# Mask blocks spread between filling units on VectorE, one core of a hybrid attention layer

## The chip, the cores and the metric

The kernel runs on one core of one Trainium2 chip. The metric is device time in microseconds (us) of one execution, lower is better. Engines are called PE (TensorE), DVE (VectorE), ACT (ScalarE), POOL (GpSimd) and SP (SyncE, which here issues every large transfer).

## The reference, cut to what matters

One decoder layer over 1024 tokens of width 1024: an input projection, two parallel attention groups (sliding window, and a sparse group "DSA" whose keys are chosen by an indexer), a cross-attention over 256 memory tokens, and an MLP. The change touches how the choice of keys becomes a mask:

```python
score = jnp.where(causal[None], score, NEG_INF)
_, idx = lax.top_k(score, topk)          # 256 of the keys
ok = idx <= t[None, :, None]
sel = jax.vmap(lambda c, i: c[i])(c_kv, idx)
logits = jnp.where(ok[:, None], logits + bias, NEG_INF)
```

and, beside it in time, the memory's keys and values, which do not depend on the layer's input:

```python
kv = mem @ wkv + bkv
k, v = jnp.split(kv, 2, axis=-1)
```

## The kernel before, in words

The kernel keeps float32 accuracy by splitting each operand of a matmul into a high part and a low part (fp32r) and issuing three matmuls (`mm3`). Weights come through `wload` (lines 148 to 176): a transfer fills a raw buffer `wr` (four of them, 256 KB each), ACT (or POOL) writes the high part into `wh` (line 172), and POOL and DVE, taking turns where `lo=(POOL, DVE)`, write the low part raw minus high into `wl` (line 173). Once both have read it, the raw buffer is free for the next load. One "pair" of memory units shares one `wload`: four raw buffers, of which POOL does the low parts of the first and third, DVE of the second and fourth.

The indexer's scores of six query blocks (n = 2 to 7, of 384 to 1024 keys) lie in `sc`. DVE finds a threshold per row, a rare repair path (`settle_all`, behind a branch) follows, and then `mask_rows` turns each block of scores into an additive mask in place, with five DVE instructions a block (lines 833 to 837): equal to the threshold, a running sum over these (the scan, line 834), at most the threshold, a comparison and a sum. Attention reads `sc` only later (line 965).

While DVE and ACT do this, PE is kept busy by a list `fill` of 60 units: projections `proj_unit` (matmuls `fill<-xT`), small ones `latent_k` (`fill<-cT`), and the memory's `mem_k`, `mem_v` (`fill<-fb,wh` and `fill<-fb,wl`, of 256 columns) and `mem_vo` (`fill<-wh,wt`). A projection's result leaves PSUM through `split_store`: ACT writes its high part (line 444), DVE its low part (line 445) into a `wt` tile (five of them), and SP stores the tile to `qa_d` or `qb_d`; `latent_k` goes through ACT (448, 449), POOL (450) and SP to `kb_d`. The tile is reused when its stores have landed.

The order in which each engine takes its instructions is fixed when the program is built: a scheduler works it out from the data, from the order of the code and from extra order edges. `follow(i, name)` adds such an edge: instruction i is put behind `latest[name]`, without a semaphore. Units 26 to 59 are emitted behind `settle_all` (`CUT = 26`); `mask_rows` is emitted once, ahead of the twentieth of these (`MASKS = 20`), and nothing tells the scheduler where in DVE's order its blocks belong.

Of the kernel before, what the change touches and what calls it, by code (L numbers as in the profile page):

```python
# [17 lines left out]
OP = mybir.AluOpType  # L18
# [9 lines left out]
NEG = -1e30  # L28
# [11 lines left out]
def kernel(ctx: ExitStack, tc: tile.TileContext, x, mem, ln_emb_g, ln_emb_b, w_in, b_in,  # L40
# [4 lines left out]
    PE, ACT, DVE, POOL, SP = nc.tensor, nc.scalar, nc.vector, nc.gpsimd, nc.sync  # L45
    x, mem, out = x[0], mem[0], out[0]
# [19 lines left out]
    def f(ap):  # L66
        return ap.bitcast(F32)
# [3 lines left out]
    def place(pl, names, shape, dt=F32):  # L71

        i = turn[names] = turn.get(names, -1) + 1
        tag = names[i % len(names)]
        return pl.tile(shape, dt, name=tag, tag=tag, bufs=4 if tag in ("wh", "wl", "wr") else 1)
# [63 lines left out]
    latest = {}  # L139

    def follow(i, *names):

        for nm in names:
            if nm in latest:
                tc.add_manual_dep(i.ins, latest[nm].ins.name, NOSYNC, reason="order")

    def wload(src, r0, nk, c0, nc_, hi=(ACT,), lo=(POOL,)):

        wh, wl = [], []
        step = min(nk, 1024 // nc_)  # L150
        for k in range(0, nk, step):
            h, l = (place(pw, w, [P, step, nc_], F32R) for w in (WH, WL))
            r = r0 + k * P
            for i in range(2):
                raw = place(pw, WR, [P, 512])
                if step == 1:
                    ws = slice(i * 512, i * 512 + 512)
                    SP.dma_start(raw, src[r:r + P, c0 + i * 512:c0 + i * 512 + 512])
                    hs, ls = h[:, 0, ws], l[:, 0, ws]
                else:  # L160
                    n2 = step // 2
                    raw = raw.rearrange("p (k c) -> p k c", k=n2)
                    part = src[r + i * n2 * P:r + (i + 1) * n2 * P, c0:c0 + nc_]
                    last_load[:] = [SP.dma_start(raw, part.rearrange("(k p) c -> p k c", p=P))]
                    hs, ls = h[:, i * n2:(i + 1) * n2], l[:, i * n2:(i + 1) * n2]
                eng = hi[i % len(hi)]
                if eng is POOL:
                    POOL.tensor_scalar(hs, raw, 1.0, 1.0, op0=OP.mult, op1=OP.mult)
                elif eng is DVE:
                    DVE.tensor_copy(hs, raw)  # L170
                else:
                    follow(ACT.activation(hs, raw, AF.Copy), "xT")  # L172
                lo[i % len(lo)].tensor_tensor(out=ls, in0=raw, in1=f(hs), op=OP.subtract)  # L173
            wh += [h[:, i] for i in range(step)]
            wl += [l[:, i] for i in range(step)]
        return wh, wl
# [225 lines left out]
    def kdup(pl, src, *names):  # L402
        kk = [place(pl, n, [P, T], F32R) for n in names]
        for hl in range(2):
            for e in range(2):
                SP.dma_start(f(kk[hl])[e * 64:e * 64 + 64], src[hl])
        return kk
# [51 lines left out]
    def proj_unit(c0, nw, cs, bias, scale, dst, t0, n):  # L459
        if cs == 0 and t0 == 0:  # L460
            FW["p"] = wload(w_in, 0, KT, c0, nw, (POOL,))
        split_store(project(*cols(FW["p"], cs), t0, n), bias, scale, dst, t0, n)
# [35 lines left out]
    def mem_proj(c):  # L498
        if c % 2 == 0:
            FW["w"] = wload(xa_wkv, 0, KT, c * P, 256, lo=(POOL, DVE))  # L500
        wh, wl = cols(FW["w"], c % 2 * P)
        p = fill_bank()
        mm3(p[:, :M], [(wh[k], wl[k], memT[k // 4][:, k % 4, 0], memT[k // 4][:, k % 4, 1]) for k in range(KT)])
        return p[:, :M]
# [21 lines left out]
    def mem_vo(h, nh, late=False):  # L526
        if late:
            vt = FW["vt"][:, h % 2]
            wh, wl = wload(xa_wo, h * 256, 2, nh * 512, 512, (POOL,))
        else:  # L530
            vt = FW["v", h]
            if nh == 0:
                FW["o"] = wload(xa_wo, h * 256, 2, 0, D, lo=(POOL, DVE))
            wh, wl = cols(FW["o"], nh * 512, 512)
        for mt in range(2):
            ms = slice(mt * P, mt * P + P)
            p = psum.tile([P, 512], F32, name="mm", bufs=2) if late else fill_bank()
            mm3(p, [(vt[:, d, 0, ms], vt[:, d, 1, ms], wh[d], wl[d]) for d in range(2)])
            o = place(pw, WR, [P, 512]) if late else wtile([P, 512], F32)
            ACT.activation(o, p, AF.Copy)  # L540
            SP.dma_start(vwo_d[h * 256 + mt * P:h * 256 + mt * P + P, nh * 512:nh * 512 + 512], o)
# [60 lines left out]
    for at, u in zip((13, 11, 10, 9, 8, 6, 5), [(open_attention,)] + [(first_loads, i) for i in range(6)]):  # L602
        fill.insert(len(fill) - at, u)

    CUT, MASKS = 26, 20
    ik = kdup(p1, ik_d, ("ikh",), ("ikl",))
    cm = p1.tile([P, P], F32, name="cm")
    DVE.memset(cm, 0.0)
# [5 lines left out]
    bound, base, need, thr, ngt = (p1.tile([P, NQ], F32, name=nm) for nm in ("bound", "base", "need", "thr", "ngt"))  # L614

    def srow(n):
        return sc[:, SCO[n]:SCO[n] + (n + 1) * P]
# [4 lines left out]
    def col(t, n):  # L622
        return t[:, n - 2:n - 1]
# [103 lines left out]
    for i in range(len(PULL)):  # L727
        for n in range(NB - 1, 1, -1):
            s = every[n]
# [11 lines left out]
    ORDER = (2, 3, 4, 5, 6, 7)  # L741
# [13 lines left out]
    some = p1.tile([1, 1], I32, name="some")  # L755
    for i, n in enumerate(ORDER):
        w = (n + 1) * P
# [65 lines left out]
                for n in range(2, NB):  # L823
                    settle(n)

    def mask_rows():
        DVE.tensor_scalar(ngt, ngt, -NEG, None, op0=OP.mult)
        for i, n in enumerate(ORDER):
            w = (n + 1) * P
            s, t = srow(n), col(thr, n)  # L830
            e, le = (p1.tile([P, 1024], F32, name="r", bufs=3) for _ in range(2))
            pre = p1.tile([P, 1024], F32, name="pre", tag=("ikh", "ikl")[i % 2], bufs=1)
            DVE.tensor_scalar(e[:, :w], s, t, -NEG, op0=OP.is_equal, op1=OP.mult)
            DVE.tensor_tensor_scan(pre[:, :w], e[:, :w], e[:, :w], ngt[:, n - 2:n - 1], OP.add, OP.bypass)
            DVE.tensor_scalar(le[:, :w], s, t, NEG, op0=OP.is_le, op1=OP.mult)
            DVE.scalar_tensor_tensor(e[:, :w], pre[:, :w], -0.5 * NEG, e[:, :w], op0=OP.is_le, op1=OP.mult)
            DVE.tensor_tensor(out=s, in0=e[:, :w], in1=le[:, :w], op=OP.add)
# [3 lines left out]
        unit(*args)  # L841
    settle_all()
    for i, (unit, *args) in enumerate(fill[CUT:]):
        if i == MASKS:
            mask_rows()
        unit(*args)
    behind.clear()
    s1.close()
# [20 lines left out]
    def parts(t):  # L869
        return t[:, :, 0], t[:, :, 1]  # L870
# [159 lines left out]
    def big(tag, shape=(P, 2, 2, 512), dt=F32R):  # L1030
        return BIG[tag].tile(list(shape), dt, name=tag, tag=tag)
# [71 lines left out]
    for half in range(2):  # L1103
        beside = []
        if half == 0:
            residual(0)
            for k in MIX_ORDER:
                t = parts(big("a%d" % (k + 1)))
# [85 lines left out]
    def split(hl, raw, lo):  # L1194
        ACT.activation(hl[:, 0], raw, AF.Copy)  # L1195
        return lo.tensor_tensor(out=hl[:, 1], in0=raw, in1=f(hl[:, 0]), op=OP.subtract)  # L1196
# [57 lines left out]
    def load_up(j):  # L1254
        raw = []
        for h in range(2):
            r = place(pr, ("row2", "row0", "row1"), [P, 4, 256])
            SP.dma_start(r, w_up[h * 512:h * 512 + 512, j * 256:j * 256 + 256].rearrange("(k p) c -> p k c", p=P))
            raw.append(r)
        return raw  # L1260
# [43 lines left out]
    for j in range(NF):  # L1304
# [5 lines left out]
        raw = ahead.pop(0) if ahead else load_up(j)  # L1310
        a11, a21, a12, a22 = (r[:, :, i * P:i * P + P] for r in raw for i in range(2))
        s2 = place(pw, WL if j >= NPRE else WR, [P, 4, P])
        op = partial(up_operand, WH if j < NPRE else ("wh", "wh", "wl"))
# [35 lines left out]
        n = 0 if j >= NPRE else 1  # L1349
# [62 lines left out]
    for c, (r0, nk, steps) in enumerate(CHUNKS):  # L1412
# [24 lines left out]
        for s, (sums, a, b, outs, done) in enumerate(steps):  # L1437
# [10 lines left out]
            for n in range(nk):  # L1448
# [5 lines left out]
                for nm, w in ((a, WH), (b, WL)):  # L1454
                    t = place(pw, w, [P, 2, 512], F32R)
                    eng = lo_engine()
                    i = split(t, R[nm][n], eng)
# [27 lines left out]
    for tb in range(NB):  # L1485
        half, i = divmod(tb, 4)
# [28 lines left out]
def _build(nc, arrays, inputs, **kw):  # L1515
    import numpy as _np
    args = []
    named = [(n, inputs[n]) for n in _INS] + [("bucket_rows", _bucket_rows())]
    for name, v in named:
        a = _np.ascontiguousarray(v)  # L1520
        arrays[f"in_{name}_dram"] = a
        args.append(nc.dram_tensor(f"in_{name}_dram", a.shape, mybir.dt.from_np(a.dtype), kind="ExternalInput").ap())
    for i, (shape, dtype) in enumerate(_OUTS):
        args.append(nc.dram_tensor(f"out_{i}_dram", shape, mybir.dt.from_np(_np.dtype(dtype)), kind="ExternalOutput").ap())
    with tile.TileContext(nc, schedule_with_timeline_sim=True) as tc:
        kernel(tc, *args, **kw)
# [11 lines left out]
```

## Time and profile before

| | |
|---|---|
| time, median of 3 runs | 1540.87 us (1537.93 to 1541.44) |
| the profiled execution's own time | 1535.34 us |
| its span, first to last instruction | 1533.6 us |
| busy PE / DVE / ACT / POOL | 1433.7 / 1092.5 / 753.1 / 764.2 us |
| granted PE clock, mean | 0.979 |

Each engine's busy time is a mean over stages of the program that differ. The stage of this change lies between 225 and 345 us of the span; a timeline of one engine there shows what ended each idle time. A busy PE need not be a fast PE: the spacing of its matmuls tells.

### The profile page before, as it was taken

What the parts mean: (1) busy time and instruction counts of PE and PEld (TensorE: products, weight loads), DVE (VectorE), ACT (ScalarE), POOL (GpSimd) and SP (SyncE); (2) the same over time, 40 slices, a digit from 0 to 9 for tenths busy, and PEclk for the clock granted to TensorE, in tenths of its full rate; (3) what the DMA queues carried; (4) which work ended last, traced back from release to release, by engine and by line L of the source; (5) the groups of instructions that cost most, each with busy time, mean ns of one, the idle gap of its engine ahead of it and who ended that gap; (6) DMA issues with size and microseconds to landing.
All of it is one profiled execution on the core that took longest, in us unless ns stands there. A gap on an engine that the chain in (4) does not pass through costs nothing. (4 is left out here: it accounts for less than half of the span.)

```text
span 1533.6 us, 21756 instructions
## 1 busy us (share of the span) xinstructions
PE 1433.7 (93%) x7190; PEld 1198.8 (78%) x7190; DVE 1092.5 (71%) x2064; ACT 753.1 (49%) x1517; POOL 764.2 (50%) x710
## 2 busy tenths in 40 slices
PE   4989998879999998999999899999999999999797
PEld 4977876868888876788888678888888887888676
DVE  6739888438878869873453775755444999999957
ACT  6537722458778843345244354455554534454222
POOL 2523433336557637566556575454444335355545
PEclk9999999999999999999999989999999999999999
DMA  5352544985494376333222134333334932410002
GB/s 182 111 170 63 160 124 130 305 259 173 140 282 142 118 254 206 109 118 109 76 90 83 42 117 148 107 124 110 110 110 134 391 137 82 150 56 14 21 30 101
DMA packets 140049, 206.62 MB, mean 135 GB/s; under 512 B 18199, under 2 KB 83230, under 8 KB 139934
## 3 DMA queue, kind: packets, MB, share of 16 engines
q1 hardware_dynamic: 139934, 205.21, 41.9%
q8 instruction: 57, 0.93, 0.3%
q14 instruction: 58, 0.48, 0.1%
HBM read 151.66 MB, written 52.45 MB: 133 GB/s over the span
## 5 line engine op out<-in xcount | busy, mean ns | idle before, releaser
L91 PE MATMUL b<-a,wh 128*128 128x512 f32 x1072 | 300.3, 402 | 9.0 <-DVE a L1182 7.9
L173 POOL TENSOR_TENSOR wl<-wr,wh 128x512 fp32r<-128x512 f32 x150 | 219.1, 1477 | 156.3 <-ACT wh L172 142.7
L91 PE MATMUL b<-wl,wh 128*128 128x512 f32 x1192 | 278.1, 392 | 12.0 <-POOL wl L1196 6.6
L91 PEld LDWEIGHTS b<-wl,wh 128*128 128x128 f32 x1192 | 224.3, 189 | 63.3 <-POOL wl L1196 7.8
L91 PEld LDWEIGHTS b<-a,wh 128*128 128x128 f32 x1072 | 204.0, 191 | 58.2 <-issue 8.7
L172 ACT ACTIVATE wh<-wr 128x512 fp32r<-128x512 f32 x144 | 85.2, 627 | 137.1 <-PE b L91 52.5
L1196 POOL TENSOR_TENSOR wh<-row,wh 128x512 fp32r<-128x512 f32 x72 | 97.6, 1360 | 92.0 <-ACT wh L1195 84.1
L91 PE MATMUL b<-wh,a 128*128 128x512 f32 (+1 forms) x416 | 122.5, 369 | 7.2 <-DVE a L866 5.2
L91 PE MATMUL fill<-xT,wh 128*128 128x512 f32 (+1 forms) x416 | 125.4, 380 | 1.0 <-ACT wt L448 0.8
L1196 POOL TENSOR_TENSOR wl<-a,wl 128x512 fp32r<-128x512 f32 x44 | 71.7, 1628 | 107.0 <-ACT wl L1195 97.6
L91 PE MATMUL b<-a,wl 128*128 128x512 f32 x400 | 123.1, 397 | 0.0
L1195 ACT ACTIVATE wh<-a 128x512 fp32r<-128x512 f32 x80 | 50.7, 634 | 114.5 <-PE b L91 92.0
L91 PEld LDWEIGHTS b<-wh,a 128*128 128x128 f32 x416 | 76.3, 191 | 22.8 <-DVE a L866 5.6
L91 PEld LDWEIGHTS fill<-xT,wh 128*128 128x128 f32 x416 | 76.3, 189 | 17.2 <-ACT wt L448 1.3
L1391 DVE TENSOR_TENSOR xr<-xr,b 128x512 f32<-128x512 f32 x132 | 81.6, 679 | 11.2 <-PE b L91 11.1
L91 PEld LDWEIGHTS b<-a,wl 128*128 128x128 f32 x400 | 75.2, 188 | 17.4
L1316 DVE TENSOR_TENSOR lt<-b,lt 128x512 f32<-128x512 f32 x80 | 53.4, 686 | 35.6 <-PE b L91 31.7
L91 PE MATMUL fill<-xT,wl 128*128 128x512 f32 (+1 forms) x208 | 78.6, 380 | 0.0
L874 DVE TENSOR_TENSOR PT<-tr,PT 128x512 fp32r<-128x512 f32 (+3 forms) x128 | 71.0, 576 | 9.1 <-ACT PT L873 8.7
L1195 ACT ACTIVATE wh<-row 128x512 fp32r<-128x512 f32 x72 | 44.9, 627 | 65.8 <-PE b L91 49.5
L91 PE MATMUL b<-wl,a 128*128 128x512 f32 (+1 forms) x208 | 76.0, 368 | 1.2 <-POOL wl L173 1.2
L1443 DVE TENSOR_TENSOR a<-a,a 128x512 f32<-128x512 f32 x84 | 70.5, 857 | 2.3 <-POOL wh L1196 1.3
(345 smaller groups left out, 3412.7 us busy)
## 6 DMA issues: line engine op xcount, KB each, us to landing
row<-in_w_up_dram SPq DMA_DIRECT2D x32, 512.0 KB, 3.8
ff_d<-lt SPq DMA_DIRECT2D x28, 512.0 KB, 3.0
a<-in_w_down_dram SPq DMA_DIRECT2D x50, 256.0 KB, 5.4
a<-ff_d SPq DMA_DIRECT2D x46, 256.0 KB, 5.4
wr<-in_xa_wkv_dram SPq DMA_DIRECT2D x32, 256.0 KB, 4.0
wr<-in_w_o_dram SPq DMA_DIRECT2D x32, 256.0 KB, 3.4
wr<-in_xa_wq_dram SPq DMA_DIRECT2D x32, 256.0 KB, 2.6
wr<-vwo_d SPq DMA_DIRECT2D x32, 256.0 KB, 2.8
```

The costliest lines, as they stand in the source:

```text
L91: i = PE.matmul(o, a, b, start=start, stop=stop)
L172: follow(ACT.activation(hs, raw, AF.Copy), "xT")
L173: lo[i % len(lo)].tensor_tensor(out=ls, in0=raw, in1=f(hs), op=OP.subtract)
L874: DVE.tensor_tensor(out=PT[1], in0=pt, in1=f(PT[0]), op=OP.subtract)
L1195: ACT.activation(hl[:, 0], raw, AF.Copy)
L1196: return lo.tensor_tensor(out=hl[:, 1], in0=raw, in1=f(hl[:, 0]), op=OP.subtract)
L1316: DVE.tensor_tensor(out=o, in0=a, in1=b, op=op)
L1391: DVE.tensor_tensor(out=xs, in0=xs, in1=p, op=op)
L1443: i = DVE.tensor_tensor(out=R[o][n], in0=R[x][n], in1=R[y][n], op=op)
```

## The change

In `wload`, the newest low part that DVE writes is remembered as `latest["lo"]`. `mask_rows` takes a list of blocks, and the first instruction of each block is put behind that low part in DVE's order. The six blocks are emitted apart, ahead of units 8, 11, 14, 17, 20 and 23 behind the cut.

```diff
-                lo[i % len(lo)].tensor_tensor(out=ls, in0=raw, in1=f(hs), op=OP.subtract)
+                on = lo[i % len(lo)]
+                one = on.tensor_tensor(out=ls, in0=raw, in1=f(hs), op=OP.subtract)
+                if on is DVE:
+                    latest["lo"] = one
...
-    CUT, MASKS = 26, 20
+    CUT, MASKS = 26, (8, 11, 14, 17, 20, 23)
...
-    def mask_rows():
-        DVE.tensor_scalar(ngt, ngt, -NEG, None, op0=OP.mult)
-        for i, n in enumerate(ORDER):
+    def mask_rows(some):
+        if some[0] == 0:
+            DVE.tensor_scalar(ngt, ngt, -NEG, None, op0=OP.mult)
+        for i in some:
+            n = ORDER[i]
...
-            DVE.tensor_scalar(e[:, :w], s, t, -NEG, op0=OP.is_equal, op1=OP.mult)
+            follow(DVE.tensor_scalar(e[:, :w], s, t, -NEG, op0=OP.is_equal, op1=OP.mult), "lo")
...
-        if i == MASKS:
-            mask_rows()
+        if i in MASKS:
+            mask_rows([MASKS.index(i)])
```

No instruction is added or taken away; the scheduler gives DVE another order. In the changed program the line numbers of the low part and of `split_store` are 1 and 3 higher, those of the masks 5 higher (line 833 is 838 there).

DVE before, from the branch of the repair path on, where the masks begin:

```order
L821 NO_OP
L827 TENSOR_SCALAR ngt<-ngt 128x6
L833 TENSOR_SCALAR r<-sc,thr 128x384
L835 TENSOR_SCALAR r<-sc,thr 128x384
L833 TENSOR_SCALAR r<-sc,thr 128x512
L834 SCALAR_TENSOR_TENSOR pre<-r,ngt 128x384
L834 SCALAR_TENSOR_TENSOR pre<-r,ngt 128x512
L836 SCALAR_TENSOR_TENSOR r<-pre,r 128x384
L836 SCALAR_TENSOR_TENSOR r<-pre,r 128x512
L837 TENSOR_TENSOR sc<-r 128x384
L445 SCALAR_TENSOR_TENSOR wt<-fill,colst,wt 128x512
```

And DVE at the same place in the changed program:

```order
L824 NO_OP
L831 TENSOR_SCALAR ngt<-ngt 128x6
L448 SCALAR_TENSOR_TENSOR wt<-fill,colst,wt 128x512 x2
L174 TENSOR_TENSOR wl<-wr,wh 128x512 x2
L838 TENSOR_SCALAR r<-sc,thr 128x384
L840 TENSOR_SCALAR r<-sc,thr 128x384
L448 SCALAR_TENSOR_TENSOR wt<-fill,colst,wt 128x512
L839 SCALAR_TENSOR_TENSOR pre<-r,ngt 128x384
L448 SCALAR_TENSOR_TENSOR wt<-fill,colst,wt 128x512
```

The first two low parts of projections and the first two low parts of memory weights now stand ahead of every mask; before, the first low part of weights stood behind 20 mask instructions.

DVE before, behind the last mask block, in the loop of the memory units (low parts of weights, and line 519, the low part of a value unit's result):

```order
L173 TENSOR_TENSOR wl<-wr,wh 128x512 x6
L519 SCALAR_TENSOR_TENSOR wt<-fill,colst,wt 128x256
L173 TENSOR_TENSOR wl<-wr,wh 128x512
L519 SCALAR_TENSOR_TENSOR wt<-fill,colst,wt 128x256 x3
```

And the corresponding piece of the changed program, with two of the five blocks that stand in this loop now (512 and 640 keys):

```order
L174 TENSOR_TENSOR wl<-wr,wh 128x512
L838 TENSOR_SCALAR r<-sc,thr 128x512
L840 TENSOR_SCALAR r<-sc,thr 128x512
L839 SCALAR_TENSOR_TENSOR pre<-r,ngt 128x512
L174 TENSOR_TENSOR wl<-wr,wh 128x512
L841 SCALAR_TENSOR_TENSOR r<-pre,r 128x512
L842 TENSOR_TENSOR sc<-r 128x512
L174 TENSOR_TENSOR wl<-wr,wh 128x512
L838 TENSOR_SCALAR r<-sc,thr 128x640
L840 TENSOR_SCALAR r<-sc,thr 128x640
L839 SCALAR_TENSOR_TENSOR pre<-r,ngt 128x640
L174 TENSOR_TENSOR wl<-wr,wh 128x512
```

The blocks of 512 to 1024 keys stand behind the 6th, 8th, 10th, 12th and 14th of DVE's 20 low parts of weights; three or five mask instructions of a block come ahead of the next low part, the rest behind it.

## Rows read from the trace of the kernel before

**Rows 1.** By stretch: busy PE, PEld, DVE, ACT, POOL; clock, DMA share, GB/s.
```profile
225.00:240.00 15.00, 15.00 (x66) 12.12 (x65) 5.93 (x12) 3.27 (x5) 1.29 (x1) 1.00 0.21 58
...
247.70:262.20 14.50, 8.13 (x49) 7.69 (x48) 14.50 (x14) 4.43 (x8) 7.02 (x5) 0.76 0.43 129
262.20:278.00 15.80, 13.30 (x72) 11.60 (x72) 12.91 (x15) 6.19 (x11) 4.53 (x4) 0.89 0.94 286
...
300.00:343.50 43.50, 35.49 (x213) 31.07 (x213) 17.43 (x29) 20.99 (x46) 15.15 (x16) 0.92 0.85 281
```

**Rows 2.** What PE waited for, 240 to 350 us (total, times, longest).
```profile
PE fill L91 <- DVE wl L173: 6.9, 2, 5.4
PE fill L91 <- ACT wh L172: 6.7, 6, 3.6
PE fill L91 <- POOL wl L173: 3.7, 5, 0.9
```

**Rows 3.** Timeline of PE (start, length, instruction, idle before and releaser).
```profile
249.04 0.39 PE L91 MATMUL fill<-fb,wl 128*128 128x256 f32 x1 [0.92 <-POOL wl L173]
...
255.47 0.58 PE L91 MATMUL fill<-fb,wl 128*128 128x256 f32 x1 [5.45 <-DVE wl L173]
255.84 0.63 PE L91 MATMUL fill<-fb,wh 128*128 128x256 f32 x2
...
256.48 0.63 PE L91 MATMUL fill<-fb,wh 128*128 128x256 f32 x2
...
259.68 0.47 PE L91 MATMUL fill<-fb,wh 128*128 128x256 f32 x2
...
260.46 0.40 PE L91 MATMUL fill<-fb,wh 128*128 128x256 f32 x2
...
260.82 0.40 PE L91 MATMUL fill<-fb,wh 128*128 128x256 f32 x2
...
270.44 0.38 PE L91 MATMUL fill<-fb,wl 128*128 128x256 f32 x1 [1.48 <-DVE wl L173]
```

**Rows 4.** Timeline of DVE, 234 to 317 us.
```profile
234.34 0.17 DVE L827 TENSOR_SCALAR ngt<-ngt 128x6 f32<-128x6 f32 x1 [6.01 <-DVEq L821]
...
239.10 0.75 DVE L445 SCALAR_TENSOR_TENSOR wt<-fill,colst,wt 128x512 fp32r<-128x512 f32 x1
...
253.67 1.75 DVE L173 TENSOR_TENSOR wl<-wr,wh 128x512 fp32r<-128x512 f32 x1
...
283.32 1.02 DVE L173 TENSOR_TENSOR wl<-wr,wh 128x512 fp32r<-128x512 f32 x1 [0.68 <-ACT wh L172]
...
314.30 1.21 DVE L173 TENSOR_TENSOR wl<-wr,wh 128x512 fp32r<-128x512 f32 x1 [2.05 <-ACT wh L172]
```

**Rows 5.** Timeline of ACT and of SP, same columns.
```profile
243.90 0.63 ACT L449 ACTIVATE wt<-wt 128x512 fp32r<-128x512 f32 x1 [10.61 <-DMA qb_d<-wt]
244.44 2.18 ACT L172 ACTIVATE wh<-wr 128x512 fp32r<-128x512 f32 x4
...
239.88 1.23 SPq L452 DMA_DIRECT2D qb_d<-wt  x2
...
249.02 10.24 SPq L164 DMA_DIRECT2D wr<-in_xa_wkv_dram  x4
```

**Rows 6.** Groups by line on DVE, 234.3 to 270 us (busy us, mean ns).
```profile
L834 DVE TENSOR_TENSOR_SCAN pre<-r,ngt 128x384 f32<-128x384 f32 (+5 forms) x6 | 11.4, 1916 | 0.0
...
L835 DVE TENSOR_SCALAR r<-sc,thr 128x384 f32<-128x384 f32 (+5 forms) x6 | 4.5, 744 | 0.0
...
L833 DVE TENSOR_SCALAR r<-sc,thr 128x384 f32<-128x384 f32 (+5 forms) x6 | 3.5, 582 | 0.0
```

**Rows 7.** POOL: two low parts beside masks; then the group, 280 to 334 us.
```profile
246.26 4.54 POOL L173 TENSOR_TENSOR wl<-wr,wh 128x512 fp32r<-128x512 f32 x2
...
L173 POOL TENSOR_TENSOR wl<-wr,wh 128x512 fp32r<-128x512 f32 x15 | 19.8, 1318 | 32.5 <-ACT wh L172 27.2 <-ACT wt L509 3.2 <-PE fill L91 2.0
```

**Rows 8.** The attention stage behind it, one stretch (columns as rows 1).
```profile
345.00:560.00 215.00, 203.27 (x1445) 185.80 (x1444) 166.01 (x573) 163.88 (x430) 128.70 (x203) 0.98 0.57 175
```

## The prediction

> **What bounds the kernel now.** I read the busy time by stretch first. Around the masks PE is the engine that loses: from 247.7 to 262.2 us it is busy 8.13 of 14.50 us at a mean granted clock of 0.76, while DVE is busy all 14.50, and the transfers run at 129 GB/s where the next stretches run at 286 and 281 [rows 1]. The list of PE's waits says on whom: 6.9 us in two waits on low parts of weights that DVE writes, 3.7 in five on those of POOL, 6.7 in six on ACT's high parts [rows 2]. PE's timeline places them: 0.92 us at 249.04 (POOL), 5.45 at 255.47 (DVE), 1.48 at 270.44 (DVE) [rows 3]. Behind the long wait PE is slow as well: one triple of 256-column matmuls begins 0.64 us after the one before (255.84, 256.48) until about 259.7, and 0.36 after it once the clock is back (260.46, 260.82) [rows 3]: the lower level, 1.2 GHz, right behind an idle PE.
>
> Then why was DVE late? Its timeline: free to go on at 234.34, it takes masks, reaches the first low part of a projection only at 239.10, and the first low part of weights at 253.67 [rows 4]. The mask instructions are 32.0 us in all (five groups of six, from 11.4 down to 3.5) [rows 6], and nobody needs their result before attention, some 80 us later. The first late low part has a second effect: SP's store of the projection goes out at 239.88, ACT's line 449 waits 10.61 us for a tile that this store frees and starts at 243.90, and ACT's four high parts of weights come only behind it, at 244.44 [rows 5]. And SP's next four loads of weights are spread over 10.24 us from 249.02 [rows 5], since each waits for a raw buffer that a late low part holds. So one order on DVE holds up ACT, SP, the transfers and PE.
>
> **The change part by part.** Instructions stay the same; only their order moves, and behind it the order of the other engines.
>
> *First low parts.* The two projection low parts now stand right behind the branch: the first at about 234.5 instead of 239.10, so 4.6 us sooner. Its store follows at 235.3, its tile is free 4.0 us later (239.88 to 243.90 in rows 5), and ACT's four high parts run from about 239.9 to 242.0 (2.18 us [rows 5]). DVE is then waiting for them, not behind masks: both its low parts are written by about 243.5, and POOL's two by 244 to 245. PE reaches these weights at about 247.7, when its projections end. So the waits of 0.92 and 5.45 us both go, and with them the slow stretch: from 255.5 to 259.7, 4.2 us, of which (0.64 - 0.36) / 0.64 = 0.44 is lost, 1.85 us. Together 8.2 us.
>
> *Second late low part.* DVE's third low part of weights stood behind the 1024-key block. It has only a projection's low part or two before it now, and its raw buffer is loaded before 250 because SP's loads no longer wait 10.24 us. I take the 1.48 us as gone, and its slow stretch: a mean clock of 0.89 over 15.80 us [rows 1] is (1 - 0.89) / 0.5 x 15.8 = 3.5 us at the low level, times 0.44, 1.5 us. Together 3.0. The waits on POOL and ACT beside it stay: they are the turn-round of a pair, not the masks.
>
> Both gains, 11.2 us, have to be fed. Transfers begin 4.6 us sooner, and the stretch 247.7 to 262.2, at 129 GB/s for 14.5 us, could move its bytes at 283 GB/s in 6.6 [rows 1]: 7.9 us. That is 12.5 us of idle transfer time against 11.2 needed, so transfers just about allow it.
>
> *Blocks in the loop.* What is late next is the loop of the memory units, 262 to 343 us: load, high part, low part, load again, with a DMA share of 0.94 to 0.85 [rows 1]. Five blocks stand in it now, three of whose parts (lines 833, 835, 834) cost 0.58 + 0.74 + 1.92 = 3.2 us a block on average [rows 6]. Ahead of the low parts that follow the blocks of 512, 640 and 1024 keys DVE idles only 0.68 to 2.05 us now (two of the three are shown) [rows 4], 1.35 on average, so each of these comes about 1.9 us later, 5.6 in all; the other two blocks fall where DVE idles for longer. Whether this reaches PE is open: PE never waits for DVE in this loop now, only in the two cases above [rows 2], so DVE's half has slack. Ends: 0 and 5.6; I take 3.0, the middle, because a late low part also holds a raw buffer and so a load.
>
> *POOL beside masks.* Two low parts of POOL that ran beside masks took 4.54 us, 2.27 each, against a mean of 1.32 for 15 of them in the loop [rows 7]: 0.95 more. Masks will fill about half of the loop's first 60 us, so some seven of the 15 may meet one. PE does wait for POOL there, but in five short waits [rows 2]. Ends: 0 and 7 x 0.95 = 6.7; I take 2.0, two of them on the path. The Trainium skill ("SBUF — State Buffer", Who interferes with whom) has VectorE and GpSimd share one pair of ports, which an instruction holds to its end while the other engine waits, for instructions with two SBUF inputs too. By that rule a POOL low part could wait for a whole scan, and this term would be up to 7 x 1.9 = 13 us, an estimate from that page; the trace agrees that both slow down, by about one microsecond.
>
> *The attention stage.* The scheduler also gives the stage from 345 to 560 us a slightly different order, with nothing added. PE is busy 203.27 of 215 us there [rows 8]; I take 0, and for the ends a quarter of its 11.7 idle us, 3 either way. What PE gained before carries through, since no transfer or clock time fixes when it starts.
>
> **Sum:** -8.2 - 3.0 + 3.0 + 2.0 = -6.2 us. Against the profiled execution's own 1535.34 us this is 1529.1; that execution lies 5.5 us below the median of the runs, 1540.87, and I forecast against the median: 1534.7.
>
> **The rivals.** *The loop has room for all of it.* DVE idles much between 280 and 340 us, and POOL's slow parts fall off the path: the full 11.2 us, 1529.7. For it: PE does not wait for DVE there. Against it: the blocks stand straight ahead of low parts, in the busiest part of DVE's new order.
>
> *The transfers absorb it.* If the loop is bound by its raw buffers' turn-round rather than by when it starts, only the earlier start of the stores counts, 4.6 us, and the terms in the loop cost 5.0: no change, 1541.3. For it: a DMA share of 0.94 to 0.85 [rows 1]. Against it: the transfers' own idle time, worked out above.
>
> *POOL is held by masks, and PE by POOL.* Slower. Place: the first and third low part of a pair, 280 to 320 us. If all seven meetings cost 0.95 and reach PE (6.7), the three delays on DVE all count (5.6), and three of the new waits bring the clock down again for 1.85 us each (5.5), the loop loses 17.8 against 11.2 won: 6.6 us slower, 1547.5. It decides where a POOL low part ends later than the slack of its pair, which is none where PE waits for POOL already. By the page on SBUF named above the price would be higher still. Against it: before, PE lost only 3.7 us to POOL in five waits, two of them away from any mask.
>
> *The change doesn't do what it says.* The edge binds the first instruction of a block alone. The printed order shows each block where it is meant to be, so I give this nothing.
>
> **How the numbers follow.** Forecast (its own range, 1531 to 1538): 0.45. Full gain: 0.18. Absorbed: 0.21. Held by POOL: 0.16. A measurement of this kernel tells about 0.2%, 3.1 us, from no change. Faster by over that: 0.45 + 0.18 plus a little of the absorbed case, 0.65. Within: 0.19. Slower: 0.16. The range reaches from the full gain with the attention stage's 3 us, 1527, to a little above the absorbed case, 1543.5; beyond it lie most of the slower case and a few hundredths below.
>
> **What would show it.** Right: DVE's first low part of weights at about 241 instead of 253.67; SP's store at about 235; no wait of PE for DVE's low parts between 247 and 262 us; a granted clock of 1.0 there; attention beginning at about 337 instead of 343.5. The blocks in the loop: low parts on DVE that start behind mask instructions instead of behind ACT, POOL low parts above 2 us between 270 and 320. Wrong: a wait of PE above 2 us for POOL or DVE between 262 and 330, or a beginning of attention that has not moved.

## The result, and the profile after

The changed kernel takes 1530.29 us, median of 10 runs (1525.85 to 1533.4), beside 1537.64 us for the kernel before in 10 runs on the same chip. The ratio is 0.9945, interval [0.9931, 0.996]: 8.5 us faster (7.4 by the medians), and all of the interval is past the 0.2% that a measurement can tell. The forecast was 6.2 us faster. The profiled execution's own time is 1526.1 us, its span 1524.3.

By stretch, in the columns of [rows 1], core 0 of the changed kernel:

```profile
247.70:262.20 14.50, 14.50 (x101) 13.42 (x100) 7.73 (x11) 5.88 (x11) 4.61 (x4) 1.00 0.92 270
262.20:278.00 15.80, 12.38 (x82) 11.26 (x82) 8.83 (x10) 6.71 (x12) 6.11 (x5) 0.89 0.80 257
278.00:300.00 22.00, 18.03 (x137) 16.55 (x136) 21.86 (x22) 8.80 (x18) 6.87 (x5) 1.00 0.90 288
300.00:343.50 43.50, 35.62 (x231) 30.81 (x230) 27.79 (x61) 24.47 (x62) 19.23 (x24) 1.00 0.85 257
```

The stretch in which PE lost most is full: 14.50 of 14.50 us busy at a granted clock of 1.00, where it was 8.13 at 0.76, and the transfers move 270 GB/s where they moved 129 [rows 1]. DVE, 14.50 busy there before, is now busy 7.73; its full stretch has moved to 278 to 300 us, 21.86 of 22. The next stretch, 262.2 to 278, did not get better: 12.38 of 15.80, 13.30 before.

How the first low parts got there, on DVE, SP and ACT of the changed kernel (line 831 is 827 of before, 174 is 173, 452 and 455 are 449 and 452):

```profile
234.47 0.17 DVE L831 TENSOR_SCALAR ngt<-ngt 128x6 f32<-128x6 f32 x1 [6.55 <-DVEq L824]
...
241.31 0.85 DVE L174 TENSOR_TENSOR wl<-wr,wh 128x512 fp32r<-128x512 f32 x1 [5.12 <-ACT wh L172]
...
243.79 1.45 DVE L838 TENSOR_SCALAR r<-sc,thr 128x384 f32<-128x384 f32 x1
```
```profile
235.56 1.23 SPq L455 DMA_DIRECT2D qb_d<-wt  x2
...
242.96 2.62 SPq L164 DMA_DIRECT2D wr<-in_xa_wkv_dram  x4
```
```profile
239.61 0.63 ACT L452 ACTIVATE wt<-wt 128x512 fp32r<-128x512 f32 x1 [6.15 <-DMA qb_d<-wt]
240.14 2.18 ACT L172 ACTIVATE wh<-wr 128x512 fp32r<-128x512 f32 x4
```

Compare with [rows 4] and [rows 5]: the store goes out 4.3 us sooner (239.88 to 235.56), ACT's high parts 4.3 sooner (244.44 to 240.14), the first low part of weights 12.4 sooner (253.67 to 241.31), and it now waits for ACT. SP's four loads are issued within 2.62 us, not spread over 10.24.

PE's waits from 230 to 350 us in the changed kernel (total, times, longest):

```profile
PE fill L91 <- DVE wl L174: 5.1, 5, 1.5
PE fill L91 <- ACT wh L172: 3.9, 5, 1.4
PE fill L91 <- POOL wl L174: 2.5, 3, 0.8
```

PE still waits 5.1 us for DVE, but in five short waits, all behind 262 us; the long one of 5.4 [rows 2] is gone, and its waits for POOL have fallen from 3.7 to 2.5.

Where the gain lies is best measured inside one profile, since the same point of the program, DVE's first instruction behind the repair path, lies up to 1.9 us apart from profile to profile (234.14 to 236.03). The two marks are PE's first matmul of the memory units (`fill<-fb`) and its first of attention (`lg<-KAh`). Before, and in the changed kernel:

```profile
247.72 0.40 PE L91 MATMUL fill<-fb,wh 128*128 128x256 f32 x2
...
331.52 0.22 PE L91 MATMUL lg<-KAh,qs 128*128 128x128 f32 x1
```
```profile
247.46 0.40 PE L91 MATMUL fill<-fb,wh 128*128 128x256 f32 x2
...
322.25 0.22 PE L91 MATMUL lg<-KAh,qs 128*128 128x128 f32 x1
```

That is 83.80 us, and 74.79 in the changed kernel: 9.0 less. I call it the length of the stage below. Behind it 2.4 us are given back: from that matmul to the last copy of `od` (line 986, 544.11; line 991, 537.28) it is 212.6 us before and 215.0 in the changed kernel (212.3 to 220.2 in the kernels of the experiments). By the end of the span the two profiles are 9.3 us apart, so I take single profiles to be good to some two microseconds.

### The profile page after: what moved, and what is told of

Same layout as the page of the kernel before. It is cut to its first block, busy times and chain, and to the rows that moved or that the text cites. A ratio compares the mean times of both kernels' runs of the same rounds, so it can differ in the third digit from the quotient of the medians.

```text
span 1524.3 us, 21763 instructions
## 1 busy us (share of the span) xinstructions
PE 1429.8 (94%) x7190; PEld 1195.2 (78%) x7190; DVE 1096.4 (72%) x2064; ACT 754.4 (49%) x1517; POOL 754.1 (49%) x710
## 5 line engine op out<-in xcount | busy, mean ns | idle before, releaser
L91 PEld LDWEIGHTS b<-a,wl 128*128 128x128 f32 x400 | 75.3, 188 | 17.3
L1212 ACT ACTIVATE lt<-lt,colst 128x512 f32<-128x512 f32 x60 | 43.3, 722 | 56.5 <-DVE lt L1321 55.5
```

The source lines that it names most:

```text
L91: i = PE.matmul(o, a, b, start=start, stop=stop)
L1212: ACT.activation(c, src, AF.Relu, bias=colst[:, C_UP + col:C_UP + col + 1])
```

## The experiments

Times are ratios to the kernel before on the same chip; a thousandth is 1.5 us.

**Undo one half of the gain: only the stores sooner.** The kernel before, with all masks put behind the second low part of a projection, and no other edit. The first low part of weights stays behind masks.

```diff
+            splits.append(one)
...
+        latest["lo"] = splits[9]
-            DVE.tensor_scalar(e[:, :w], s, t, -NEG, op0=OP.is_equal, op1=OP.mult)
+            follow(DVE.tensor_scalar(e[:, :w], s, t, -NEG, op0=OP.is_equal, op1=OP.mult), "lo")
```

> The kernel before with one order edge: all mask blocks are emitted where they were, but behind the second low part of a projection on VectorE. So the two stores of projections leave some 4.6 us sooner, as in the change, while the first low part of weights still stands behind 18 mask instructions. Theory A (the first low parts of weights are what counts; PE's wait of 5.45 us ends with them): the masks begin 1.4 us later than before, so PE's long wait at about 248 us stays, 5 to 7 us long, and the time is within 3 us of before, ratio 0.998 to 1.002. Rival B (the earlier stores, and with them ACT and the transfers, are what counts): 4.6 us faster, ratio 0.997 or below, with the long wait much shorter.

Measured: 1535.58 us, 0.9978 [0.9964, 0.9993], 3.4 us faster; the stage is 82.88 us long, 0.9 less. PE's waits, 240 to 350 us, and the first late one:

```profile
PE fill L91 <- ACT wh L172: 7.7, 5, 2.9
PE fill L91 <- POOL wl L173: 4.5, 4, 2.4
PE fill L91 <- DVE wl L173: 3.7, 4, 2.1
```
```profile
250.54 0.38 PE L91 MATMUL fill<-fb,wl 128*128 128x256 f32 x1 [2.09 <-DVE wl L173]
```

The long wait for DVE shrinks from 5.45 to 2.09 us, since the first low part of weights comes at 249.80, between masks still. Neither theory came as told: the wait is far shorter than A's 5 to 7 us, and the time lies between A's range and B's. Stage and ratio differ here: a tenth of the change's gain by the one profile, 40% by the twelve runs, which I trust more (1.1 to 5.5 us by the interval). By both, more than half of the gain needs the low parts of weights themselves ahead of the masks.

**The masks in one row, early or late.** The changed kernel with all six blocks given out together, nearly in a row with low parts of weights between them: behind DVE's second low part of weights (early), or behind the twelfth (late).

```diff
-    CUT, MASKS = 26, (8, 11, 14, 17, 20, 23)
+    CUT, MASKS = 26, (20, 20, 20, 20, 20, 20)
```

The early one also stops `latest["lo"]` at the second low part.

> The change with one edge instead of six: all six blocks are emitted where they were before, ahead of the twentieth unit, and only put behind the second low part of weights. The masks then run nearly in a row on VectorE, some 32 us from about 243 us on, with the low parts of the next pairs between them. Theory A (the first two low parts give 8.2 us, the third 3.0, spreading costs up to 5): PE's waits of 0.92 and 5.45 us are gone; the third to sixth low parts come late, so a wait of PE for VectorE of 1 to 4 us appears between 258 and 275 us; 5 to 8 us faster than before, ratio 0.995 to 0.997. Rival C (it is the spreading over many units that counts): a stall of over 5 us only moves from 250 to about 260 us, and the time is within 3 us of before.

> The change with all six blocks behind the twelfth low part of weights: the loop of memory units up to about 292 us holds no mask at all, and the 32 us of masks run from there to about 330 us between the last low parts. Theory A (low parts of weights late means PE late, wherever the masks stand): the gain of about 9 us at 290 us is kept, then PE waits for VectorE's low parts of the output weights 3 to 6 us in all, and attention's first blocks, which need their masks, wait too: 2 to 6 us faster than before, slower than the change. Rival D (where the masks stand does not matter once the first two low parts are ahead of them): like the change, ratio 0.9945 within 0.002.

Measured: early 1533.65 us, 0.9972 [0.9958, 0.9987]; late 1534.97 us, 0.9984 [0.9967, 1.0001]; the stage is 80.05 and 79.82 us long. Both give away about half of the gain or more (4.2 and 6.0 of 8.5 us), at different places. Early lies between its two theories (5 to 8 us faster, or within 3), late is as theory A had it (2 to 6 us), though its interval just reaches no change. Early, PE's timeline has two waits that the change has not:

```profile
265.28 0.58 PE L91 MATMUL fill<-fb,wl 128*128 128x256 f32 x1 [3.81 <-DVE wl L174]
...
276.06 0.39 PE L91 MATMUL fill<-fb,wl 128*128 128x256 f32 x1 [2.26 <-DVE wl L174]
```

Late, the front is as good as in a kernel without masks, and the row stands in DVE's way in the last stretch, DVE busy 38.94 of 43.50 us:

```profile
247.70:262.20 14.50, 14.50 (x99) 13.33 (x98) 5.58 (x8) 6.50 (x12) 5.17 (x4) 1.00 0.94 299
262.20:278.00 15.80, 12.97 (x101) 12.12 (x100) 4.62 (x5) 7.54 (x14) 5.41 (x6) 1.00 0.81 253
...
300.00:343.50 43.50, 33.89 (x195) 28.20 (x195) 38.94 (x55) 19.17 (x46) 21.05 (x17) 0.93 0.82 236
```

The stretch from 262.2 to 278 us without masks (the kernel below), for comparison; the change has 12.38 at a clock of 0.89 there:

```profile
262.20:278.00 15.80, 13.13 (x102) 12.20 (x100) 4.35 (x5) 6.60 (x12) 5.37 (x5) 1.00 0.81 255
```

So the change has two parts, and both count: the first low parts ahead of the masks, and the masks spread over the loop and not in one row.

**What the masks cost where they stand now.** The changed kernel with no call of `mask_rows` in the loop, so that attention reads raw scores where it should read masks.

```diff
-        if i in MASKS:
-            mask_rows([MASKS.index(i)])
```

> The change without the masks: the blocks' instructions (lines 836 to 842 and the scaling of ngt) are left out, so attention reads raw scores where it should read masks. It prices what the masks still cost in their new places. By the prediction's terms (3.0 us on VectorE and 2.0 on POOL): 5 us faster than the change, about 13 us faster than before, ratio 0.991. If the loop hides them (rival of the full gain): 0 to 2 us faster than the change, ratio 0.9935 to 0.9945. If POOL is held by masks: POOL's low parts fall from a mean of 1.44 us to 1.29 and the time by over 6 us.

Measured: 1527.59 us, 0.9931 [0.9906, 0.9956]. That is 0.0014 or 2.2 us below the change, well inside the two intervals, and between what the prediction's terms (0.991) and the full gain (0.9935 to 0.9945) would give. PE's waits, 240 to 350 us:

```profile
PE fill L91 <- ACT wh L172: 6.6, 6, 2.7
PE lg L91 <- DMA wl<-kb_d: 3.9, 2, 2.7
PE fill L91 <- POOL wl L174: 2.5, 3, 0.8
...
PE fill L91 <- DVE wl L174: 0.2, 1, 0.2
```

The 5.1 us of waits for DVE go to 0.2, and in their place PE waits 6.6 for ACT's high parts (3.9 in the change): many of the weights are no sooner there. The stage, in this profile:

```profile
248.98 0.28 PE L91 MATMUL fill<-fb,wh 128*128 128x256 f32 x1
...
321.93 0.22 PE L91 MATMUL lg<-KAh,qs 128*128 128x128 f32 x1
```

72.95 us, 10.9 less than before and 1.8 less than the change. So 37.8 us of masks on DVE (the groups below) cost about 2 us where they now stand, by the stage and by the ratio alike; the ratios alone would allow anything from none to 6.6 us.

**More work in the same places.** Every mask instruction but the last of a block issued twice, and, apart from that, only the scan twice (the same values both times); beside the second the changed kernel once more, against the same runs of the kernel before.

```diff
+            for _ in range(2):
+                follow(DVE.tensor_scalar(e[:, :w], s, t, -NEG, op0=OP.is_equal, op1=OP.mult), "lo")
...
```

> The changed kernel in which the first four instructions of each block are issued twice in the same place (the same result is computed twice): about 29 us more work for DVE in the loop, all of it straight ahead of low parts. Theory A (slack in DVE, POOL hardly held): 0 to 4 us slower than the change, ratio 0.9945 to 0.997; PE's waits for DVE low parts rise from 5.1 us to under 10; POOL's low parts stay below 1.8 us on average (1.44 in the change). Theory B (the prediction's price: 3.0 on the path for the 3.2 us a block that is in the way, plus 2.0 for POOL): about 5 us slower than the change, ratio near 0.998. Theory C (the rival in which POOL is held by masks and PE by POOL): 10 us or more slower than the change, ratio above 1.001, POOL low parts of 2.3 us and more on average beside masks, and PE's waits for POOL above 8 us where the change has 2.5.

> The changed kernel with only the scan of each mask block issued twice (the same result), about 11 us more work for DVE in the loop, where masks_twice had about 29 and became 12.6 us slower than the change. Theory A (DVE has no slack left behind the change, each further microsecond on it costs 0.4): about 5 us slower than the change, ratio near 0.9975, PE's waits for DVE low parts near 8 us. Theory B (DVE's slack ends somewhere above the change's amount of work, and masks_twice fell off that edge): within 2 us of the change, ratio 0.996 or less, PE's waits for DVE near the change's 5.1.

> The changed kernel once more, to stand beside the other two on the same chip. All theories: a ratio within 0.0015 of 0.9945, and a profile whose first low part of weights on DVE comes near 241 and whose attention begins within 2 us of 322.25; what the two profiles of the same kernel differ by is what a single profile can't tell.

| | masks on DVE, us | PE waits for DVE / POOL, us | stage, us | ratio | interval |
|---|---|---|---|---|---|
| no masks | 0 | 0.2 / 2.5 | 72.95 | 0.9931 | [0.9906, 0.9956] |
| the change | 37.8 | 5.1 / 2.5 | 74.79 | 0.9945 | [0.9931, 0.996] |
| the change again | 36.0 | 4.0 / 3.3 | 75.23 | 0.9949 | [0.9931, 0.9966] |
| scan twice | 48.2 | 8.3 / 4.3 | 79.18 | 0.9966 | [0.9952, 0.9981] |
| masks twice | 64.8 | 14.7 / 2.5 | 83.48 | 1.0027 | [1.0011, 1.0042] |

The work is the sum of the five mask lines on DVE; the waits are those of 240 to 350 us. These are the groups of the change from 234 to 345 us, of which [rows 6] are the counterpart, with the low parts of weights and the idle time before them:

```profile
L174 DVE TENSOR_TENSOR wl<-wr,wh 128x512 fp32r<-128x512 f32 x20 | 20.0, 1002 | 23.3 <-ACT wh L172 23.2
L839 DVE TENSOR_TENSOR_SCAN pre<-r,ngt 128x384 f32<-128x384 f32 (+5 forms) x6 | 11.1, 1847 | 0.0
L842 DVE TENSOR_TENSOR sc<-r 128x384 f32<-128x384 f32 (+5 forms) x6 | 8.8, 1462 | 0.2
L841 DVE SCALAR_TENSOR_TENSOR r<-pre,r 128x384 f32<-128x384 f32 (+5 forms) x6 | 6.8, 1131 | 0.0
L840 DVE TENSOR_SCALAR r<-sc,thr 128x384 f32<-128x384 f32 (+5 forms) x6 | 6.6, 1094 | 0.0
...
L838 DVE TENSOR_SCALAR r<-sc,thr 128x384 f32<-128x384 f32 (+5 forms) x6 | 4.5, 750 | 0.0
```

The row of low parts without masks, and with masks twice, the same stretch:

```profile
L174 DVE TENSOR_TENSOR wl<-wr,wh 128x512 fp32r<-128x512 f32 x20 | 20.9, 1047 | 44.0 <-ACT wh L172 43.8
```
```profile
L174 DVE TENSOR_TENSOR wl<-wr,wh 128x512 fp32r<-128x512 f32 x20 | 19.0, 948 | 16.5 <-ACT wh L172 16.5
```

DVE's idle time ahead of its 20 low parts falls as masks are added: 44.0 us without them, 23.3 in the change, 16.5 with masks twice. And the price of a microsecond of masks rises: 2.2 us for the first 37.8 (0.06 each), 12.6 for the next 27.0 (0.47), by the differences of the ratios times 1538; their uncertainty leaves at most 0.18 for the first and at least 0.34 for the rest. Scan twice divides the rest into 3.2 us for 10.4 and 9.4 for 16.6, which the intervals don't tell apart. The length of the stage grows by 1.8, 4.4 and 4.3 us; what masks twice loses beyond it, it loses in attention, whose first units find DVE still at the masks (its last compare starts at 334.66): 220.2 us to the last copy of `od`, 215.0 in the change.

The sum of the idle time doesn't rank the kernels, though. It is 28.4 us with the masks in one row late and 28.7 before, more than the change's 23.3, and both are slower; the place of the idle time counts. What does follow the length of the stage, over all eleven profiles, is the sum of PE's waits in it for the three producers of weights (DVE, ACT and POOL): 9.3 us without masks (the shortest stage), 10.2 and 11.5 in the change, 11.9 and 13.9 with the blocks sooner (below), 13.8 with scan twice, 14.7 and 13.7 in one row early and late, 15.9 with stores first, 16.1 with masks twice and 17.3 before (the longest). The stage less these waits is 63.3 to 67.4 us.

No theory of masks twice had the size by its own mechanism: slack (0 to 4 us) and the prediction's price (5) were both too low; the 10 or more were expected only of POOL held by masks, and POOL was not it. PE's waits for POOL stay at 2.5 us, and POOL's low parts take 1.65 us on average, not 2.3; what rose is the waits for DVE, from 5.1 to 14.7. Scan twice lies between its two theories: 2.6 us above the change by the ratios against the same runs of the kernel before, 3.5 by the medians. The change again came as expected in its time; its first low part of weights (242.84) and its attention (324.13) are both late by the 1.5 to 1.9 us by which the profile as a whole is.

```profile
L174 POOL TENSOR_TENSOR wl<-wr,wh 128x512 fp32r<-128x512 f32 x19 | 27.5, 1448 | 42.1 <-ACT wh L172 35.4 <-PE fill L91 6.7
```
```profile
L174 POOL TENSOR_TENSOR wl<-wr,wh 128x512 fp32r<-128x512 f32 x17 | 28.1, 1654 | 43.0 <-ACT wh L172 43.0
```

(POOL, 244 to 330 us: the change, then masks twice.)

**The blocks sooner.** Idle time of DVE that can take masks may as well be used sooner; in the change DVE idles 4.51 and 3.49 us ahead of its fifth and sixth low part. Two ways of giving the blocks out:

```diff
-    CUT, MASKS = 26, (8, 11, 14, 17, 20, 23)
+    CUT, MASKS = 26, (8, 8, 8, 10, 11, 14)
```

and `(8, 8, 10, 11, 14, 17)`, one step milder.

> The changed kernel with its blocks given out earlier, ahead of units 8, 8, 8, 10, 11 and 14 behind the cut: three blocks stand between DVE's 2nd and 3rd low part of weights, one each behind the 5th, 7th and 9th, none from the 10th on. Theory A (the loop is bound by loads and their turn-round, the masks are nearly free wherever each low part is not kept waiting for more than a block or two): a ratio to the kernel before within 0.002 of the change's 0.9945; attention begins within 1 us of the change's 322.25; PE's waits for DVE low parts move to the front of the loop (the 3rd low part, behind three blocks) and stay under 4 us in all, as the 5.1 us of the change. Theory B (as the prediction had it: the blocks in the later loop cost 3 to 5 us on PE's path): up to 3 us faster than the change, ratio 0.9925 or less, attention beginning near 319.5. Theory C (DVE's 3rd low part is as critical as its first): 2 to 4 us slower than the change, ratio 0.996 to 0.997, with a PE wait for DVE of over 2 us between 260 and 280.

> The changed kernel with its blocks ahead of units 8, 8, 10, 11, 14 and 17: two blocks between DVE's 2nd and 3rd low part of weights, one behind the 4th, 6th, 8th and 10th, so none stands in the last third of the loop, and the 3rd low part waits for two blocks and not for three as in blocks_earlier. Theory A (the masks cost the change next to nothing): ratio within 0.002 of the change's. Theory B (the 2.7 us between the change and the kernel without masks is their cost, and DVE's idle time ahead of the 3rd, 5th and 6th low part can take it): ratio 0.993 or less, PE's waits for DVE under 3 us.

Measured: 1527.99 us, 0.9931 [0.9916, 0.9946], and 1532.92 us, 0.9952 [0.9935, 0.997]. Neither is told apart from the change (0.9945 and 0.9949), and the milder one doesn't lie between the other two; the stage, 76.62 and 78.30 us, is rather longer than the change's 74.79. So this gave no version that is shown to be better, as theory A had it in time; its waits for DVE (under 4 us) were too low. PE's waits change their place and nearly keep their sum: with the blocks at (8, 8, 8, 10, 11, 14),

```profile
262.87 0.39 PE L91 MATMUL fill<-fb,wl 128*128 128x256 f32 x1 [1.42 <-DVE wl L174]
...
273.20 0.58 PE L91 MATMUL fill<-fb,wl 128*128 128x256 f32 x1 [3.20 <-DVE wl L174]
```

5.8 us in three waits for DVE, against 5.1 in five, with the last one at 288.75.

## Why the prediction was right, and where its sizes were off

The sign and the mechanism came as told: 8.5 us faster by the ratio, 6.2 forecast; the median, 1530.29, lies in the range and just below the forecast's own (1531 to 1538). Of the 4.4 us between it and 1534.7, 3.2 are the kernel before: the forecast counted from 1540.87, the median of 3 runs, where 10 runs gave 1537.64.

- *First low parts, -8.2: right in its signs; its size was not measured alone.* First low part of weights at 241.31 (about 241 forecast), store at 235.56 (235), no wait of PE for DVE between 247 and 262 us, clock 1.00 there. With *stores first* the halves are seen apart: up to 3.4 us come from the early stores.
- *Third low part, -3.0: right in the sum, not where I put it.* The wait of 1.48 us for DVE at 270.44 [rows 3] went, but PE's stretch from 262.2 to 278 is no better than before, at the same clock of 0.89. More was won ahead of it (the first of the memory's keys leaves PSUM through ACT at 255.76, line 512, instead of 268.34, line 509: 12.6 us) and some of it lost again there (the third, at 269.00 instead of 276.48, is 7.5 us sooner): PE now waits there for ACT's high parts (1.33 us) and POOL's low parts (0.85, 0.84). Both terms together, -11.2, agree with the kernel without masks: 10.9 us by the stage, 10.6 by the ratio (6.8 to 14.5 by its interval).
- *Blocks in the loop, +3.0, and POOL beside masks, +2.0: the step that was mis-sized.* Together 5.0 us were charged; measured, the masks in their new places cost 1.8 us of the stage (2.3 in the second profile of the change) and 2.2 by the ratios, the latter with an uncertainty that takes in both 0 and 5. Part of the charge on DVE fell on waits that PE has anyway, for ACT's high parts: 6.6 us without masks, 3.9 in the change. The charge on POOL had next to no case. It counted seven meetings of 0.95 us, two of them on the path; between 270 and 320 us one of POOL's low parts took more than 2 us:

```profile
306.98 2.08 POOL L174 TENSOR_TENSOR wl<-wr,wh 128x512 fp32r<-128x512 f32 x1 [1.81 <-ACT wh L172]
```

Their mean, 244 to 330 us, rose from 1.42 to 1.45, and PE's waits for POOL fell from 3.7 to 2.5 us (3.3 in the second profile of the change; 2.5 with masks twice, 4.3 with scan twice). Sum -11.2 + 2 instead of -11.2 + 5 gives -9.2, and the stage came out 9.0 shorter; that it fits so closely is luck, since single profiles are good to some two microseconds.

- *The loop has room for all of it* (11.2 us) is not far off. The change's interval ends at 10.6 us faster, but the change and the kernel without masks are not told apart by their ratios; that the masks still cost something rests on the stages of two profiles, 1.8 and 2.3 us.
- *Transfers absorb it* falls: the gain shrinks in the loop, from 12.6 us at the first key to 7.5 at the third, and is 9.3 where attention begins: not to nothing.
- *POOL held by masks* falls by masks twice, which was slower than before, for DVE's sake. I had the place and the sign of the danger, and the wrong engine: with more masks PE's waits for DVE rise, 5.1 to 14.7 us, not those for POOL.
- *Attention, 0 within 3: right in size.* It gave back 2.4 us by its last copy of `od`, no more than the kernels of the experiments differ by there; the cause stays open. PE's waits in attention before (331.52 to 544.11 us), and then in the changed kernel (322.25 to 537.28):

```profile
PE lg L91 <- DMA wl<-kb_d: 5.8, 6, 2.3
...
PE lg L91 <- DMA wh<-kb_d: 0.5, 1, 0.5
...
PE lg L91 <- DVE sm L901: 0.3, 1, 0.3
```
```profile
PE lg L91 <- DMA wl<-kb_d: 4.3, 3, 2.1
...
PE lg L91 <- DVE sm L970: 1.8, 3, 0.9
PE lg L91 <- DVE sm L906: 1.3, 1, 1.3
...
PE lg L91 <- DMA wh<-kb_d: 1.2, 3, 0.6
```

The waits for the keys that SP loads (`kb_d`) did not grow, 6.3 us before and 5.5 after. Those for DVE's sums (`sm`) did, from 0.3 to 3.1 (4.6 in the second profile of the change); no run changed them alone.

- *Attention beginning at about 337 instead of 343.5: a wrong mark.* At 343.5 of before stands the end of a wait inside attention, not its beginning:

```profile
343.55 0.30 PE L91 MATMUL lg<-wl,qs 128*128 128x128 f32 x1 [2.35 <-DMA wl<-kb_d]
```

Its first matmul stands at 331.52 before and at 322.25 in the changed kernel: 9.3 us sooner, where the forecast had 6.5.

## What to carry to other kernels

Work without a near due time belongs behind the producers that a busy engine waits for, and spread between them: in one row, early or late, the same instructions gave away about half of the gain or more. Its price isn't a price per microsecond: here it was small for the masks there are (about 2 us for 37.8), and per microsecond about eight times that for what was added. The total of the engine's idle time doesn't show it; the waits of the engine that bounds the stage, added up over all its producers, followed the length of the stage from kernel to kernel. Doubling the moved work is a cheap way to learn how near the edge a schedule stands.

## What the runs showed of the hardware

The same 30 mask instructions took 32.0 us in one row [rows 6] and 37.8 spread over the loop (36.0 in its second profile), since more of them met instructions of POOL: by the timelines, 5 of the 30 ran over 0.3 us longer than the shortest of their shape before, 11 in the change, and in none of the ten profiles with masks did one do so without a POOL instruction at the same time. I had charged such meetings to POOL alone; DVE pays as well. POOL's low parts in the change, then two compares of 384 keys beside POOL, and the first compare again with masks twice, where POOL is idle:

```profile
241.57 3.44 POOL L174 TENSOR_TENSOR wl<-wr,wh 128x512 fp32r<-128x512 f32 x2
```
```profile
243.79 1.45 DVE L838 TENSOR_SCALAR r<-sc,thr 128x384 f32<-128x384 f32 x1
...
245.16 1.44 DVE L840 TENSOR_SCALAR r<-sc,thr 128x384 f32<-128x384 f32 x1
```
```profile
250.30 0.42 DVE L839 TENSOR_SCALAR r<-sc,thr 128x384 f32<-128x384 f32 x1
```

1.45 against 0.42 us, one microsecond more for an instruction that reads one tile; the first slow one ends at 245.24, POOL's second low part at 245.01. The Trainium skill ("SBUF — State Buffer", Who interferes with whom) says that a `tensor_scalar` in the mode that takes both ports locks POOL out or is locked out itself, to the end of the other's instruction. The trace agrees in size: the extra 1.03 us is less than the 1.32 us that one of POOL's low parts takes on average [rows 7]. In which mode the compare ran, no row tells.
